# A decoder layer on one core: second norm, key choice and up products rearranged

## The chip, the cores and the metric

The kernel runs on 1 core of a Trainium2 chip (trn2). The metric is the device time of one execution in microseconds (us); the time before is the median of three runs. One execution was also taken by the hardware profiler, and all rows below come from its trace. Engines: PE is TensorE's matmul, PEld its weight load, DVE is VectorE, ACT ScalarE, POOL GpSimd, SP SyncE.

## The reference

One layer over 256 tokens of width 2048, in float32. The part that matters here is what follows the token mixer:

```python
x = x + gate1 * token_mixer(h, ...)
h = rmsnorm(x, norm2_g[l]) * (1.0 + scale2) + shift2
x = x + gate2 * peer(h, peer_w_q[l], peer_sub_keys[l], peer_w_up[l], peer_w_down[l])

def peer(h, w_q, sub_keys, w_up, w_down):
    qp = (h @ w_q).reshape(B, S, 8, 2, 128)
    s = jnp.einsum('bshpe,hpne->bshpn', qp, sub_keys)
    v1, i1 = lax.top_k(s[..., 0, :], 16)
    v2, i2 = lax.top_k(s[..., 1, :], 16)
    cand = (v1[..., :, None] + v2[..., None, :]).reshape(B, S, 8, 256)
    top, ci = lax.top_k(cand, 16)
    e1 = jnp.take_along_axis(i1, ci // 16, axis=-1)
    e2 = jnp.take_along_axis(i2, ci % 16, axis=-1)
    idx = e1 * 128 + e2
    g = jax.nn.softmax(top, axis=-1)
    # per token: y = sum over its 128 experts of g * gelu(h . w_up[idx]) * w_down[idx]
```

The second factors of the modulation, scale2 and shift2, come from a product of the conditioning vector with w_ada.

## The kernel before, in words

Weights are streamed: a unit of 1 MB is loaded by SyncE into one of four buffers and split in two halves. Each half is cast by ScalarE to a high part (`split_a`, L84), VectorE or GpSimd takes the low part (`split_b`, L88), and TensorE multiplies high by high, high by low and low by high. `Stream.run` writes the order out by hand: the cast of a half is issued three halves ahead of its product. One product half is a tick; `st.at(d, f)` issues f d ticks later, ahead of that tick's product, and `st.spread` hands small steps to VectorE between ticks, as many as a budget allows. Every engine works through its queue in the order of issue.

**Second norm.** `out_done(n)` ends block n of the output projection: VectorE makes the new residual, ScalarE its sum of squares (L960). The turning of a block to columns, `tr` (L967 to L975), ends in ScalarE copies of PSUM to x1T; that of block 3 is kept as `x1c["last"]`. After the stream has been drained, `h2_start` finishes the factor A2, and `h2` sums the squares (L1021), takes the root on ScalarE (L1022) and the reciprocal, and spreads it over the partitions by a product with ones (L1029, L1031). `chunks(q)` then scales two columns blocks (L1039, VectorE), adds the bias on ScalarE (L1042, the high part) and takes the low part on VectorE (L1044). Chunks 0 and 1 come first, then `x1c["last"]`, then chunks 2 and 3; the others follow one pair a tick. After that the PSUM pool of the first phase is closed and that of the second opened over it; the query products (L1101 to L1105) write to the latter.

**Queries and keys.** `open_p2`, six ticks on, lets GpSimd issue the DMA of the keys (L1069). Query block n has 8 halves of 24 matmuls; `q_done` copies it out. After block 0, `keys_t` turns the keys on TensorE (L1083, 16 transposes through two PSUM buffers, copied out by ScalarE, L1084), and `scores` multiplies queries by keys (L1125), which starts the background search for the 16 largest.

**Key choice.** In `topk`, for each token half, each key half q and each half of the heads, VectorE compares the chosen place's key number with 0 to 15 (L1208), multiplies the result with the key indices (L1211) and sums over the last axis (L1213). Both operations have 1024 two-byte elements a partition. Meanwhile the up products of quarter 0 run: for each half VectorE turns the weights (L1255), ScalarE casts, GpSimd takes the low part.

**Up products.** `up_unit(q, r)` is one row of 128 experts in two halves of 8 column blocks. For q of 0 and 1, `mm` issues three matmuls of 256 columns for each block (L1270 to L1272), two rows share one PSUM tile, and `up_done` applies gelu straight from it. For q of 2 and 3, `mm_wide` multiplies the high weights with high and low activations in one matmul of 512 columns (L1282) and the low weights in one of 256 (L1287); `add_up` copies one half of the PSUM tile out on ScalarE (L1297) and adds the other on VectorE (L1300) before gelu. In quarter 1 the first 18 rows (`nsolo`) run alone, and the other 14 alternate with the down products of quarter 0.

Of the kernel before, what the change touches and what calls it, by code (L numbers as in the profile page):

```python
# [13 lines left out]
AF = mybir.ActivationFunctionType  # L14
OP = mybir.AluOpType
# [51 lines left out]
def layer_kernel(ctx, tc, x, c, norm1_g, norm2_g, w_ada, b_ada, w_in, conv_dw, conv_db, conv_ln_g,  # L67
                 conv_ln_b, w_conv_out, b_conv_out, q_norm_g, k_norm_g, w_attn_o, w_out, peer_w_q,
                 peer_sub_keys, peer_w_up, peer_w_down, out):
    nc = tc.nc  # L70
# [168 lines left out]
    st = Stream()  # L239
# [25 lines left out]
    eps_col = consts.tile([P, 1], F32, name="eps_col")  # L265
# [36 lines left out]
    A2 = consts.tile([P, NK], F32, name="A2")  # L302
# [60 lines left out]
    ssq = pc1.tile([P, 2], F32, name="ssq")  # L363
# [332 lines left out]
    def gate_done(which, ch):  # L696
# [4 lines left out]
                                    gate_b[which][:, 4 * ch:4 * ch + 4], op=OP.add)  # L701
        return done

    def mod2_done(dst, bias_at, ch):
        rows32 = slice(32 * ch, 32 * ch + 32)

        def done(acc):
            ps = tt_([P, NK], "mod2ps")
            for j in range(NK):
                nc.tensor.matmul(ps[rows32, j:j + 1], lhsT=acc[:, 0, 32 * j:32 * j + 32], rhs=ones[:, 0:1],  # L710
                                 start=True, stop=True)
            nc.vector.tensor_tensor(dst[rows32, :], ps[rows32, :], cols[rows32, bias_at:bias_at + 16], op=OP.add)
        return done

    gate_b = [cols2[:, 48:64], cols2[:, 64:80]]
# [231 lines left out]
    def out_done(n):  # L947
        view = lambda v: v.rearrange("p (i j l) -> p j i l", i=4, j=4)
        of_row = lambda v: v.rearrange("p (i n j l) -> p n j i l", i=4, n=4, j=4)[:, n]

        def done(z):
            og = []
            for t in range(2):

                o = t2k("og")
                ov = o.rearrange("p (j i l) -> p j i l", i=4, j=4)
                nc.vector.tensor_tensor(ov, view(z[t]), of_row(mT["g1"]), op=OP.mult)
                nc.vector.tensor_tensor(ov, ov, of_row(x1c["t"][:, t]), op=OP.add)
                junk = wk.tile([P, 512], F32, name="junk2", tag="yc")
                nc.scalar.activation(junk, o, AF.Square, accum_out=ssq2[:, t, n:n + 1])  # L960
                nc.gpsimd.dma_start(x1_dram[:, t, n * 512:(n + 1) * 512], o)
                og.append(o)
            if n == 0:
                for i in range(2):
                    x1c[i] = wk.tile([P, 8, T], F32, name="x1T", tag="c8" + "bc"[i])

            def tr():  # L967
                for m in range(2):
                    pt = tt_([P, 2, T], "px")
                    for kk in range(2):  # L970
                        for t in range(2):
                            nc.tensor.transpose(pt[:, kk, t * P:(t + 1) * P],
                                                og[t][:, (2 * m + kk) * P:(2 * m + kk + 1) * P], ident)
                    at = 4 * (n % 2) + 2 * m
                    nc.scalar.copy(x1c[n // 2][:, at:at + 2, :], pt)  # L975
            if n < 3:
                st.at(2, tr)
            else:
                x1c["last"] = tr
        return done  # L980
# [34 lines left out]
    def h2_start():  # L1015
        nc.vector.tensor_scalar(A2, A2, 1.0, None, op0=OP.add)
        nc.vector.tensor_tensor(A2, A2, cols[:, 64:80], op=OP.mult)

    def h2():
        r2 = pc1.tile([P, 2], F32, name="r2")  # L1020
        nc.vector.tensor_reduce(r2, ssq2, axis=AX, op=OP.add)  # L1021
        nc.scalar.activation(r2, r2, AF.Sqrt, scale=1.0 / D, bias=eps_col)  # L1022
        nc.vector.reciprocal(r2, r2)

        diag = wk.tile([P, T], F32, name="diag", tag="ln", bufs=2)
        for t in range(2):
            nc.vector.tensor_scalar(diag[:, t * P:(t + 1) * P], ident, r2[:, t:t + 1], None, op0=OP.mult)
        pr = tt_([P, T], "rms")
        nc.tensor.matmul(pr, lhsT=ones, rhs=diag, start=True, stop=True)  # L1029
        rr = wk.tile([P, T], F32, name="rrow", tag="ln", bufs=2)  # L1030
        nc.scalar.copy(rr, pr)  # L1031

        qh["t"] = main.tile([P, NK, 2, T], F32R, name="h2", tag="hT")
        qh["hi"], qh["lo"] = qh["t"][:, :, 0], qh["t"][:, :, 1]

        def chunks(q):
            tmp = t2k("h2t").rearrange("p (c t) -> p c t", c=2)
            for c in range(2):
                nc.vector.scalar_tensor_tensor(tmp[:, c], x1c[(q + c) // 8][:, (q + c) % 8, :], A2[:, q + c:q + c + 1], rr,  # L1039
                                               op0=OP.mult, op1=OP.mult)  # L1040
            for c in range(2):
                nc.scalar.activation(qh["hi"][:, q + c, :], tmp[:, c], AF.Identity, bias=B2[:, q + c:q + c + 1])  # L1042
            for c in range(2):
                nc.vector.scalar_tensor_tensor(qh["lo"][:, q + c, :], tmp[:, c], B2[:, q + c:q + c + 1],  # L1044
                                               qh["hi"][:, q + c, :].bitcast(F32), op0=OP.add, op1=OP.subtract)

        for q in range(0, NK, 2):
            if q == 2:
                x1c["last"]()
            if q < 4:  # L1050
                chunks(q)
            else:
                st.at(q // 2 - 2, lambda q=q: chunks(q))
        ps0.close()
        T2["ps"] = p2.enter_context(tc.tile_pool(name="psq", bufs=1, space=PSUM))
        T2["psy"] = p2.enter_context(tc.tile_pool(name="psy", bufs=1, space=PSUM))

        def rest():
            pm.close()
            p1.close()  # L1060
            open_p2()
        st.at(6, rest)
# [50 lines left out]
    def q_done(n, ps):  # L1113
        scr = T2["scr"]
        qpT = scr[:, 4096:8192].rearrange("p (a t) -> p a t", a=16)
        for b in range(2):
            nc.scalar.copy(qpT[:, 4 * n + 2 * b:4 * n + 2 * b + 2, :], ps[b])
        if n == 0:
            st.at(1, keys_t)

        def scores():
            for t in range(2):
                pt = T2["ps"].tile([P, 4, P], F32, name="sps", tag="m", bufs=2)
                for a in range(4):
                    nc.tensor.matmul(pt[:, a, :], lhsT=qpT[:, 4 * n + a, t * P:(t + 1) * P],  # L1125
                                     rhs=T2["keysT"][:, (4 * n + a) * P:(4 * n + a + 1) * P], start=True, stop=True)
                nc.scalar.copy(scr[:, t * 2048 + n * 512:t * 2048 + (n + 1) * 512], pt.rearrange("p a n -> p (a n)"))
            st.spread(topk_keys(n))
            if n == 3:
                st.spread(topk_gen)  # L1130
        st.at(3, scores)


    def top16(rows_, cost):
# [27 lines left out]
    def topk():  # L1162
        scr = T2["scr"]
        small, big = (T2["pool"].tile([P, 768], F32, name=f"small{i}", tag="ohg", bufs=2) for i in range(2))
        iota16 = small[:, 0:128].bitcast(BF).rearrange("p (a k) -> p a k", a=16)
        nc.gpsimd.iota(iota16, pattern=[[0, 16], [1, 16]], base=0, channel_multiplier=0,
                       allow_small_or_imprecise_dtypes=True)
        idb = small[:, 128:256].bitcast(BF).rearrange("p (g a) -> p g a", a=TOPK)
        cab = small[:, 256:384].bitcast(BF).rearrange("p (q h a) -> p q h a", q=2, a=TOPK)
# [7 lines left out]
        for t in range(2):  # L1177
# [26 lines left out]
            i4 = idb.rearrange("p (h q) a -> p h q a", q=2)  # L1204
            shape = [P, H8 // 2, TOPK, TOPK]
            for q in range(2):
                for hs in halves:
                    nc.vector.tensor_tensor(eq[:, hs], cab[:, q, hs, :, None].to_broadcast(shape),  # L1208
                                            iota16[:, None, :, :].to_broadcast(shape), op=OP.is_equal)
                    yield 0.7, 0  # L1210
                    nc.vector.tensor_tensor(pr[:, hs], eq[:, hs], i4[:, hs, q, None, :].to_broadcast(shape), op=OP.mult)  # L1211
                    yield 1.2, 0
                    nc.vector.tensor_reduce(ee[:, q, hs], pr[:, hs], axis=AX, op=OP.add)  # L1213
                    yield 1.2, 0
# [23 lines left out]
    def up_unit(q, r, pool_lo):  # L1238
# [11 lines left out]
        for n in range(2):  # L1250
# [55 lines left out]
                    st.at(1, add)  # L1306

            h.a, h.b, h.mm = a, b, mm
            if q >= 2:
                h.mm = mm_wide  # L1310
                if n == 1:
                    h.after = [add_up]
            elif n == 1 and r % 2 == 1:
                h.after = [lambda: up_done(q, r - 1, C["ps"])]
            u.halves.append(h)
        return u

    NT = 8  # L1320
# [6 lines left out]

    def up_rows(q, r):

        if q == 2:  # L1330
            return c_row(q, r, 2).rearrange("p (r t) -> p r t", r=2)
        return T2["pool"].tile([P, 768], F32, name="hrow", tag="ohg", bufs=2)[:, 0:512].rearrange("p (r t) -> p r t", r=2)
# [25 lines left out]
    def weigh(upto):  # L1358
        while late and late[0][0] < upto:
            late.pop(0)[1]()  # L1360
# [204 lines left out]
    some = lambda r, n: n == 1 and r % 2 == 1  # L1565
    add_units([up_unit(0, r, busy) for r in range(EQ)])
    mark_up1 = len(st.halves)
    nsolo = 18
    solo = [up_unit(1, r, busy) for r in range(nsolo)]
    for u in solo:  # L1570
        for h in u.halves:
# [43 lines left out]
    st.run(mark_h2)  # L1615
    st.flush()
    st.finish()
    h2_start()
    h2()
    st.run(mark_up)  # L1620
    st.rate = 1.35
# [44 lines left out]
```

## Time and profile before

| | us |
|---|---|
| median of three runs | 2495.65 (2494.63 to 2496.32) |
| the profiled execution | 2495.79 |
| its span, first to last instruction | 2494.0 |

The page of the profile gives the busy time of each engine and the costliest groups of instructions. The view of stretches gives the busy time by engine in a window, then the granted clock of TensorE, the busy share of the DMA engines and their rate. In the timeline each row is a start and a duration in us, the engine, the line, the operation and its tiles, and in brackets how long the engine had been idle and what ended that. A matmul's recorded duration overlaps the next one's, so the pace of matmuls is read from their starts.

### The profile page before, as it was taken

To read this page: it belongs to the slowest core of one execution; us is meant where nothing else is said; L and a number is where in the kernel's file an instruction comes from. 1 tells how busy PE (TensorE), PEld (TensorE's weight loads), DVE (VectorE), ACT (ScalarE), POOL (GpSimd) and SP (SyncE) were. 2 spreads that over 40 slices of the span, in tenths; PEclk is the share of its full clock that TensorE was granted. 3 is DMA by queue.
4 is the path that set the end of the run, shared out by engine and by line. 5 is a ranking of instruction groups with operands and counts; after the bars stand their busy time and mean duration, and the time that the engine had idled before them with its cause. 6 is when DMAs were issued, how large, how long until landed. Compare 5 with 4: busy or idle time off the path is not lost.

```text
span 2494.0 us, 37872 instructions
## 1 busy us (share of the span) xinstructions
PE 2420.0 (97%) x14704; PEld 2007.3 (80%) x14704; DVE 1874.4 (75%) x2706; ACT 1141.0 (46%) x1540; POOL 525.5 (21%) x262
## 2 busy tenths in 40 slices
PE   7999999999999899988999999999999999999998
PEld 4677877777777799888889988888877888888877
DVE  2655788787564589897998777888899777776766
ACT  5333544444434444343335555555443444455454
POOL 1000000000000008776642233322000111133023
PEclk9999999999999899999999999999999999999999
DMA  9887457677898768676557876899844687766553
GB/s 332 299 304 253 152 203 260 246 272 248 285 289 242 162 158 185 149 162 143 119 136 215 231 225 190 225 235 232 213 142 145 177 198 182 187 193 220 187 201 118
DMA packets 261172, 518.62 MB, mean 208 GB/s; under 512 B 16400, under 2 KB 57568, under 8 KB 260352
## 3 DMA queue, kind: packets, MB, share of 16 engines
q1 hardware_dynamic: 258912, 507.61, 69.8%
q0 software_dynamic: 2048, 8.58, 1.0%
q8 instruction: 115, 1.88, 0.3%
q14 instruction: 65, 0.53, 0.1%
q10 hardware_dynamic: 32, 0.01, 0.0%
HBM read 511.94 MB, written 4.19 MB: 207 GB/s over the span
## 4 chain that ended last, share of the span: by engine, by line
PE 81%; DVE 8%; POOL 1%; issue 1%; ACT 1%; DMA 0%; DVEq 0%; SPq 0%; POOLq 0%; ACTq 0%
PE aps L1282 9%; PE y L1484 6%; PE y L1485 6%; PE y L1487 6%; PE z L429 5%; PE z L431 5%; PE z L430 5%; PE aps L1287 5%; PE z L1485 3%; PE z L1484 3%; PE z L1487 3%; PE aps L1272 3%; PE aps L1270 3%; PE aps L1271 3%; PE ada L330 2%; DVE wt L1255 2%
## 5 line engine op out<-in xcount | busy, mean ns | idle before, releaser
L88 DVE TENSOR_TENSOR lo<-raw,hi 128x1024 fp32r<-128x1024 f32 x456 | 560.1, 1233 | 318.7 <-issue 92.0
L84 ACT CAST hi<-raw 128x1024 fp32r<-128x1024 f32 x504 | 526.9, 1052 | 483.4 <-DMA raw<-in_w_in_dram 92.5
L84 ACT CAST hi<-wt 128x1024 fp32r<-128x1024 f32 x256 | 269.3, 1052 | 443.1 <-DVE wt L1255 427.5
L88 POOL TENSOR_TENSOR lo<-wt,hi 128x1024 fp32r<-128x1024 f32 x116 | 290.6, 2511 | 609.4 <-PE aps L1287 420.4
L1282 PE MATMUL aps<-h,hi 128*128 128x512 f32 x1024 | 362.4, 399 | 0.0
L1255 DVE STREAM_TRANSPOSE wt<-raw 128x1024 f32<-128x1024 f32 x256 | 315.3, 1235 | 26.5 <-POOL lo L88 21.3
L1272 PE MATMUL aps<-h,lo 128*128 128x256 f32 x1024 | 293.3, 286 | 11.8 <-POOL lo L88 11.8
L1270 PE MATMUL aps<-h,hi 128*128 128x256 f32 x1024 | 295.8, 289 | 0.0
L1271 PE MATMUL aps<-h,hi 128*128 128x256 f32 x1024 | 292.2, 285 | 0.0
L1467 DVE TENSOR_TENSOR ccl<-C,cch 128x256 fp32r<-128x256 f32 x248 | 197.0, 796 | 112.3 <-PE z L1487 59.1
L1287 PE MATMUL aps<-h,lo 128*128 128x256 f32 x1024 | 277.2, 281 | 0.0
L1484 PE MATMUL y<-hi,cch 128*128 128x512 f32 x608 | 241.1, 397 | 0.0
L1485 PE MATMUL y<-lo,cch 128*128 128x512 f32 x608 | 236.9, 390 | 0.0
L1282 PEld LDWEIGHTS aps<-h,hi 128*128 128x128 f32 x1024 | 190.3, 188 | 42.7 <-issue 0.2
L1272 PEld LDWEIGHTS aps<-h,lo 128*128 128x128 f32 x1024 | 198.9, 194 | 13.8 <-POOL lo L88 13.8
L1270 PEld LDWEIGHTS aps<-h,hi 128*128 128x128 f32 x1024 | 199.0, 194 | 1.2 <-ACT hi L84 0.5
L1271 PEld LDWEIGHTS aps<-h,hi 128*128 128x128 f32 x1024 | 199.3, 195 | 0.5
L1287 PEld LDWEIGHTS aps<-h,lo 128*128 128x128 f32 x1024 | 193.3, 189 | 6.3 <-issue 0.2
L88 DVE TENSOR_TENSOR lo<-wt,hi 128x1024 fp32r<-128x1024 f32 x140 | 175.3, 1255 | 19.3 <-PE aps L1287 12.2
L1487 PE MATMUL y<-hi,ccl 128*128 128x512 f32 x608 | 187.5, 389 | 0.0
L88 POOL TENSOR_TENSOR lo<-raw,hi 128x1024 fp32r<-128x1024 f32 x48 | 116.9, 2435 | 247.4 <-PE z L1485 125.2
L1462 ACT CAST cch<-C 128x256 fp32r<-128x256 f32 x248 | 99.8, 403 | 122.0 <-PE z L1485 103.4
(304 smaller groups left out, 4530.5 us busy)
## 6 DMA issues: line engine op xcount, KB each, us to landing
raw<-in_peer_w_up_dram SPq DMA_DIRECT2D x512, 256.0 KB, 5.8
raw<-in_peer_w_down_dram SPq DMA_DIRECT2D x128, 1024.0 KB, 5.2
raw<-in_w_ada_dram SPq DMA_DIRECT2D x86, 1024.0 KB, 6.9
raw<-in_w_in_dram SPq DMA_DIRECT2D x73, 1024.0 KB, 6.9
raw<-in_w_out_dram SPq DMA_DIRECT2D x64, 256.0 KB, 5.0
raw<-in_peer_w_q_dram SPq DMA_DIRECT2D x64, 256.0 KB, 6.2
raw<-in_w_in_dram SPq DMA_DIRECT2D x22, 512.0 KB, 9.1
raw<-in_w_ada_dram SPq DMA_DIRECT2D x20, 512.0 KB, 4.9
```

Source lines behind the costliest of these rows:

```text
L84: nc.scalar.copy(h.hi, src)
L88: eng.tensor_tensor(h.lo, src, h.hi.bitcast(F32), op=OP.subtract)
L1255: nc.vector.transpose(wt.rearrange("p j g a -> p g j a"), u.raw.rearrange("p (g j a) -> p g j a", g=4, a=32)[:, :, n * 8:(n + 1) * 8, :])
L1270: nc.tensor.matmul(z, lhsT=hi[:, jj], rhs=qh["hi"][:, j, :], start=j == 0, stop=False)
L1271: nc.tensor.matmul(z, lhsT=hi[:, jj], rhs=qh["lo"][:, j, :], start=False, stop=False)
L1272: nc.tensor.matmul(z, lhsT=lo[:, jj], rhs=qh["hi"][:, j, :], start=False, stop=j == NK - 1)
L1282: wide = lambda: nc.tensor.matmul(z.rearrange("p a t -> p (a t)"), lhsT=hi[:, jj], rhs=qh["t"][:, j].rearrange("p a t -> p (a t)"), start= ...
L1287: nc.tensor.matmul(z[:, 0], lhsT=lo[:, jj], rhs=qh["hi"][:, j, :], start=False, stop=False, skip_group_check=True)
L1467: nc.vector.tensor_tensor(cl, row, ch, op=OP.subtract)
L1484: nc.tensor.matmul(z, lhsT=ch, rhs=hi, start=first, stop=False)
L1485: nc.tensor.matmul(z, lhsT=ch, rhs=lo, start=False, stop=False)
L1487: nc.tensor.matmul(z, lhsT=cl, rhs=hi, start=False, stop=last)
```

## The change

`h2_start` is called when the last of the four A2 chunks is done, in `mod2_done`, and no longer after the drain. After block 2 of the output projection, ScalarE takes the root of a constant, so that the table for roots is loaded there. Chunks 0 and 1 of the norm go through all three steps one after the other, in place of step by step together. The turning of the keys is due three ticks after block 0 and no longer one, the scores of block 0 four ticks after it and no longer three. In the key choice the compare has the places innermost, the key number being the outer axis; the multiplication reads in that order and writes with the last two axes exchanged, so the sum reads as before. Rows 18 to 31 of quarter 1 use the wide product, whose sums land in the H buffer.

```diff
@@ mod2_done
+    mod2_left = [4, 4]
             nc.vector.tensor_tensor(dst[rows32, :], ps[rows32, :], cols[rows32, bias_at:bias_at + 16], op=OP.add)
+            if dst is A2:
+                mod2_left[0] -= 1
+                if mod2_left[0] == 0:
+                    h2_start()
@@ out_done
+            if n == 2:
+                nc.scalar.activation(ssq[:, 0:1], eps_col, AF.Sqrt)
@@ h2
-        def chunks(q):
+        def chunks(q, one=False):
             tmp = t2k("h2t").rearrange("p (c t) -> p c t", c=2)
-            for c in range(2):
+            if one:
+                for c in range(2):
+                    part(tmp, q, (c,))
+            else:
+                part(tmp, q, range(2))
+
+        def part(tmp, q, cc):
+            for c in cc:
                 nc.vector.scalar_tensor_tensor(tmp[:, c], x1c[(q + c) // 8][:, (q + c) % 8, :], A2[:, q + c:q + c + 1], rr,
                                                op0=OP.mult, op1=OP.mult)
-            for c in range(2):
+            for c in cc:
                 nc.scalar.activation(qh["hi"][:, q + c, :], tmp[:, c], AF.Identity, bias=B2[:, q + c:q + c + 1])
-            for c in range(2):
+            for c in cc:
                 nc.vector.scalar_tensor_tensor(qh["lo"][:, q + c, :], tmp[:, c], B2[:, q + c:q + c + 1],
                                                qh["hi"][:, q + c, :].bitcast(F32), op0=OP.add, op1=OP.subtract)
...
-                chunks(q)
+                chunks(q, q == 0)
@@ q_done
-            st.at(1, keys_t)
+            st.at(3, keys_t)
...
-        st.at(3, scores)
+        st.at(4 if n == 0 else 3, scores)
@@ topk
-        nc.gpsimd.iota(iota16, pattern=[[0, 16], [1, 16]], base=0, channel_multiplier=0,
+        nc.gpsimd.iota(iota16, pattern=[[1, 16], [0, 16]], base=0, channel_multiplier=0,
...
-                    nc.vector.tensor_tensor(eq[:, hs], cab[:, q, hs, :, None].to_broadcast(shape),
-                                            iota16[:, None, :, :].to_broadcast(shape), op=OP.is_equal)
+                    nc.vector.tensor_tensor(eq[:, hs], cab[:, q, hs, None, :].to_broadcast(shape),
+                                            iota16[:, None].to_broadcast(shape), op=OP.is_equal)
                     yield 0.7, 0
-                    nc.vector.tensor_tensor(pr[:, hs], eq[:, hs], i4[:, hs, q, None, :].to_broadcast(shape), op=OP.mult)
+                    nc.vector.tensor_tensor(pr[:, hs].rearrange("p h k a -> p h a k"), eq[:, hs],
+                                            i4[:, hs, q, :, None].to_broadcast(shape), op=OP.mult)
@@ up_unit
-            if q >= 2:
+            if q >= 2 or (q == 1 and r >= nsolo):
                 h.mm = mm_wide
@@ up_rows
+        if q == 1:
+            weigh(r - 14)
+            return C["H"][:, r % 16:r % 16 + 2]
@@ the order at the end
-    h2_start()
+    assert mod2_left[0] == 0
     h2()
```

## Rows read from the trace of the kernel before

**Rows 1.** The page: busy time by engine; the casts of the stream.

```profile
PE 2420.0 (97%) x14704; PEld 2007.3 (80%) x14704; DVE 1874.4 (75%) x2706; ACT 1141.0 (46%) x1540; POOL 525.5 (21%) x262
...
L84 ACT CAST hi<-raw 128x1024 fp32r<-128x1024 f32 x504 | 526.9, 1052 | 483.4 <-DMA raw<-in_w_in_dram 92.5
```

**Rows 2.** Stretches: window, length, busy PE, PEld, DVE, ACT, POOL, clock, DMA.

```profile
820.00:830.00 10.00, 4.09 (x15) 2.92 (x14) 5.89 (x16) 5.61 (x12) 1.08 (x2) 0.69 0.76 175
1060.00:1120.00 60.00, 53.53 (x432) 52.00 (x431) 56.49 (x88) 24.33 (x26) 46.20 (x19) 1.00 0.70 159
1300.00:1400.00 100.00, 100.00 (x631) 90.94 (x630) 83.15 (x82) 54.59 (x76) 24.81 (x15) 1.00 0.78 228
```

**Rows 3.** Timeline of the norm; then the table load of the attention roots, by line.

```profile
823.17 1.28 ACT L1022 ACT_TABLE_LOAD   x1
823.19 0.16 DVE L1021 TENSOR_REDUCE r<-ssq 128x2 f32<-128x8 f32 x1 [0.55 <-ACT junk L960]
...
827.26 0.88 DVE L1039 SCALAR_TENSOR_TENSOR h2t<-x1T,A,rrow 128x256 f32<-128x256 f32 x2 [1.78 <-ACT rrow L1031]
...
828.33 0.88 DVE L1044 SCALAR_TENSOR_TENSOR h<-h2t,B,h 128x256 fp32r<-128x256 f32 x2 [0.18 <-ACT h L1042]
828.60 1.05 ACT L975 COPY x1T<-px 128x512 f32<-128x512 f32 x2
...
829.70 0.29 PEld L1101 LDWEIGHTS qp<-h,hi 128*128 128x128 f32 x1 [1.57 <-ACT x1T L975]
...
L493 ACT ACT_TABLE_LOAD  x1: 1283/1283/1283, 283.3 to 283.3; - x1
```

**Rows 4.** Timeline around the turning of the keys; its sequencer's wait, by line.

```profile
850.46 1.18 POOL L1069 DMA_DIRECT2D C<-in_peer_sub_keys_dram  x1 [27.29 <-DVE h L1044]
...
857.45 0.28 PE L1105 MATMUL qp<-h,lo 128*128 128x256 f32 x1
863.26 3.73 PE L1083 MATMUL kt<-ident,C 128*128 128x128 f32 x16 [5.53 <-issue]
866.64 0.56 PE L1101 MATMUL qp<-h,hi 128*128 128x256 f32 x1
...
868.21 0.28 PE L1103 MATMUL qp<-h,hi 128*128 128x256 f32 x1
...
L1083 PEldq EVENT_SEMAPHORE  x4: 51/51/7452, 855.4 to 863.1; - x4
```

**Rows 5.** Timeline: narrow and wide products; the add, by line (min/median/max ns).

```profile
1426.14 0.28 PE L1270 MATMUL aps<-h,hi 128*128 128x256 f32 x1
...
1431.54 0.28 PE L1270 MATMUL aps<-h,hi 128*128 128x256 f32 x1
...
1599.94 0.40 PE L1282 MATMUL aps<-h,hi 128*128 128x512 f32 x1
...
1605.60 0.40 PE L1282 MATMUL aps<-h,hi 128*128 128x512 f32 x1
...
L1300 DVE TENSOR_TENSOR C<-aps,C x32: 409/415/420, 1575.5 to 1831.2; 128x256 f32<-128x256 f32 x32
```

**Rows 6.** Timeline of one choice (GpSimd alone, then merged); waits in 1000 to 1120.

```profile
1016.10 1.23 DVE L1255 STREAM_TRANSPOSE wt<-raw 128x1024 f32<-128x1024 f32 x1
1016.28 2.35 POOL L88 TENSOR_TENSOR lo<-wt,hi 128x1024 fp32r<-128x1024 f32 x1 [2.92 <-PE aps L1271]
...
1016.28 5.70 POOL L88 TENSOR_TENSOR lo<-wt,hi 128x1024 fp32r<-128x1024 f32 x2 [2.92 <-PE aps L1271]
1017.25 2.47 DVE L1208 TENSOR_TENSOR C<-small 128x1024 bf16<-128x1024 bf16 x1
1019.75 2.78 DVE L1211 TENSOR_TENSOR C<-C,small 128x1024 bf16<-128x1024 bf16 x1
...
1024.71 1.22 DVE L1255 STREAM_TRANSPOSE wt<-raw 128x1024 f32<-128x1024 f32 x1
...
PE aps L1272 <- POOL lo L88: 11.8, 9, 1.9
```

More of the change, by code (lines that the diff above doesn't have):

```diff
@@ L1316, in up_unit @@
         return u
+    nsolo = 18
     NT = 8
@@ L1567, in layer_kernel @@
     mark_up1 = len(st.halves)
-    nsolo = 18
     solo = [up_unit(1, r, busy) for r in range(nsolo)]
```

## The prediction

> **What bounds the kernel now.** I read the page first: TensorE is busy for 97% of the span, VectorE for 75% and ScalarE for 46% [rows 1]. So time can be won only where TensorE stands idle or runs slowly, or by giving it less to do. The view of stretches says where to look [rows 2]. In 820 to 830 us, the second norm, TensorE is busy for 4.09 of 10 us, at a granted clock of 0.69; in 1060 to 1120 us, where the top 16 are chosen, it loses 6.5 of 60 us while VectorE is busy for 56.5. In 1300 to 1400 us, where the rows that become wide lie, it is busy throughout: there only less work on TensorE counts. The timeline adds a pause of 5.5 us at 863 us, ahead of the turning of the keys [rows 4]. The change touches all four places. Times below are of the profiled execution, 2495.8 us with 2494.0 of span; it stands 0.1 us above the median, so its sum is also the median's.
>
> **The norm: root table early, chunks one by one.** On the chain [rows 3], ScalarE, done with its last sum of squares, loads the table for the root from 823.17 to 824.45, and the root follows at about 824.47. The sum that it needs (L1021) ends at 823.35. With the table loaded after block 2, the root can start about 0.05 us after that, at 823.40: 1.07 us won. The load itself moves to a stretch where ScalarE has time (46% busy in all [rows 1]); casts run three halves ahead of TensorE there, so I cost it at nothing, or 1.28 us if that lead were gone. Squares of block 3 follow it: in the attention part a single load [rows 3] serves the twelve roots that `qk_done` takes (L493), with Squares between them, so no second load is due. The two steps that finish A2 (16 columns each) stand on VectorE ahead of L1021, which waits for ScalarE's sum anyway; moving them to the last A2 chunk is worth 0, and there they stand between ordinary VectorE work.
>
> The chunks then give the gain back. What the first weight load of the queries waits for is not chunk 0 but the copies of x1T out of PSUM: it starts at 829.70, 0.05 us after these end at 829.65 [rows 3]. On ScalarE the copies are queued behind the bias step of chunk 1. Now VectorE scales chunks 0 and 1 back to back at 827.26 and about 827.66. One by one, it scales chunk 0, waits for ScalarE's bias step, takes the remainder of chunk 0 at 828.33 and only then, some 0.40 us later (0.88 us for a pair less 0.48 for one), scales chunk 1, at 828.73: 1.07 us later than now. The bias step of chunk 1, the copies behind it and the first weight load all move with it. So 1.07 - 1.07 = 0 for the whole norm; the bounds are -1.1 (the load doesn't really wait for the copies) and +0.4 (one more VectorE step ahead of the copies).
>
> **Keys turned later.** The ninth half of the query product ends at 857.57 (its last matmul starts at 857.45), and the turning of the keys starts only at 863.26. Its sequencer waits for 7.45 us from 855.4, until about 862.9, for the keys: GpSimd issues their DMA at 850.46, after VectorE has read the last old tile [rows 4]. The turning then runs slowly until 866.64, and so do the next products: seven starts from there to 868.21 take 1.57 us where 0.12 each [rows 5] makes 0.84. So 857.57 to 866.64 is 9.07 us, and with the slow start 9.8. The change lets two halves (24 x 0.12 = 2.88 us each) run first: 857.57 + 5.76 = 863.33, just behind the landing. Nothing issued before 863 us moves: the next release of a weight buffer would come after 864. Then the turning runs warm: 16 transposes of about 0.11 us, with a pause for the copies (two buffers; 0.53 us each by the pair of the same size in [rows 3]), which now stand behind a cast of 1.05 us on ScalarE, by its mean on the page (1052 ns [rows 1]). I get 1.05 + 0.53 + 0.1 = 1.7 us to the third group, and two groups of 0.5 with a short wait: 2.7 us. 9.8 - 2.7 = **7.1 us won**. If the keys land 1 us later, 6.1; if the copies never hold TensorE up, 8.0. The scores of block 0 come one half later behind the stream but some 4 us earlier by the clock; the background work of VectorE that they start has room before block 1's scores. Who waits behind the turning is TensorE alone.
>
> **Wide up products.** A half of 24 narrow products starts at 0.36 us for each three, and the wide form at about 0.354 us for each two: from 1426.14 to 1431.54 there are 15 threes (5.40 us), from 1599.94 to 1605.60 sixteen twos (5.66 us, so 15 of them 5.31) [rows 5]. That is 0.006 us x 16 x 14 rows = 1.4 us. Added are 14 copies on ScalarE, which has time, and 14 adds on VectorE (0.42 us, one operand in PSUM) [rows 5]: 5.9 us of VectorE in some 170 us in which it is about 83% busy [rows 2]. The cover is its free sixth, so I cost them at nothing; without it they would cost 5.9. **1.2 us won** after a little for the first rows; bounds 1.6 won and, without the cover, 4.5 lost, which nothing here points to.
>
> **The key choice.** This is the large unknown. Eight times (two token halves, two keys, two halves of the heads) VectorE compares (L1208), multiplies (L1211) and sums. Both operations read two operands from SBUF and wait for the GpSimd subtraction in progress, and the next subtraction waits for them. In the group at 1017.25 [rows 6] the compare waits for the subtraction that started at 1016.28 and lasts 2.35, until 1018.63, and runs until 1019.72, 1.09 us; the next subtraction follows it; the multiplication waits for that, until 1021.98 (the two end 5.70 after 1016.28), and ends at 1022.53, a run of 0.55 us. The two runs show the rates: the compare repeats one operand along its innermost axis and takes 1.06 ns an element, the multiplication has unit steps and takes 0.53. The group from 1016.10 to 1024.71, 8.6 us, holds two halves of 2.88 us of TensorE, and TensorE waits for GpSimd's remainder in each (11.8 us in nine waits in 1000 to 1120 us [rows 6]). VectorE is the bound in these groups, so a change of its own run falls on TensorE in full, eight times.
>
> After the change the compare has unit steps: 0.55 us. The multiplication repeats its index operand and, in addition, writes 16 places apart, two bytes at a time. Call its run P. The sum is 8 x (0.55 + P - 1.09 - 0.55) = 8 x (P - 1.09). The ends: 0.55 (today's multiplication; -4.3 us) and 2.78 (the longest time that one took here, wait included; +13.5 us). The nearest row is the compare of today, 1.09, but that has one operand off unit steps and a dense output, and the new multiplication has two off. The one row that compares such forms shows a doubling for one; I take a doubling for each: P = 2.13, **8.3 us lost**. That the waits shift with the shorter compare adds some 2 us either way.
> [...]
>
> **Sum.** 0 - 7.1 - 1.2 + 8.3 = 0.0: 2495.8 us, no change. About 5 us (0.2%) is what a measurement of this kernel can tell from none.
>
> **Rivals.**
> 1. The scattered write costs nothing extra: P = 1.09, the compare and the multiplication only change places. Then -7.1 - 1.2 = -8.3, 2487.5 us. [...] It decides below P = 1.5 (8 x 0.41 = 3.3, net -5).
> 2. Slower, by the write alone: from P = 2.75 on, 8 x 1.66 = 13.3 outweighs 8.3 by 5 us: 2501 us. For it: GpSimd is held off for all of P, and its subtraction is next on the path of every half. Against it: nothing of this size is seen in a run of VectorE here.
> 3. Slower, by the keys: the keys' DMA shares the engines with the weight loads, and lands with TensorE's progress rather than by the clock. If 5.5 us of the wait stays, net is -1.6 - 1.2 + 8.3 = +5.5: 2501.3 us. Against it: no load is issued earlier than now before the keys have landed.
> 4. The norm doesn't do what it says, or does: 0 is my sum, -1.1 the gain without the chunks' delay; 2494.7 us.
>
> **How the numbers follow.** The forecast (P from 1.5 to 2.75, with rival 4 in it) has 0.53; rival 1 has 0.30; rivals 2 and 3 have 0.12 and 0.05. So faster by over 0.2% 0.30, within it 0.53, slower 0.17. The forecast's own range is 2490.8 to 2500.8 us. The range of 8 in 10 takes in the time of rival 1 (2487.5, with half a microsecond for its other terms) and reaches on the other side to 2502.
>
> **What would show it.** Right: the new multiplication runs about 2.1 us beyond the end of GpSimd's operation, the compare 0.55; TensorE's waits for GpSimd's remainder in 1000 to 1120 us grow from 11.8 to about 20 us; no idle time before the turning of the keys, and 7 us less in 853 to 876 us; the first weight load of the queries still at 829.7, right behind the copies of x1T, though the root is at 823.4. Wrong: a multiplication of 1.1 us beyond the wait (then 2487), or a first weight load near 828.6. Idle time before the turning, or TensorE waits in 1300 to 1475 us, would say that the keys or the wide rows were mis-sized.

## The result, and the profile after

The changed kernel takes 2515.1 us (median of six runs, 2513.0 to 2517.7), the kernel before 2496.0 beside it: a ratio of 1.0083, interval 1.0070 to 1.0095. It is 19 us slower; 2495.8 was forecast, with 2502 as the upper end. One of the six runs of the kernel before took 9864 us and the other five 2492.0 to 2498.0, so that its median is hardly moved by the one. The profiled execution took 2512.95 us, 2511.2 of it span, and so lies 2.2 us below the median.

The busy line of the page of after, beside [rows 1]:

```profile
PE 2425.3 (97%) x14480; PEld 2002.1 (80%) x14480; DVE 1903.4 (76%) x2720; ACT 1145.1 (46%) x1555; POOL 535.0 (21%) x262
```

TensorE has 224 matmuls fewer, as meant, and VectorE is busy for 29 us longer. The two stretches of after that hold the norm and the choice, beside [rows 2] (window, length, busy time of each engine, clock, DMA):

```profile
820.00:830.00 10.00, 4.11 (x16) 2.92 (x15) 5.75 (x14) 4.32 (x11) 1.08 (x2) 0.70 0.92 209
1060.00:1120.00 60.00, 51.55 (x384) 50.58 (x383) 57.66 (x94) 21.93 (x24) 48.57 (x17) 0.91 0.68 156
```

In 1060 to 1120 us TensorE gets through 384 matmuls where it had 432, at a granted clock of 0.91 where it was 1.00, and VectorE is busy for 57.66 of the 60 us. One key choice of after, on the timeline of VectorE, GpSimd and ScalarE in turn, and under them TensorE's waits in 1000 to 1120 us (total us, times, longest), beside [rows 6]. L1272 turns weights, L1224 is the compare, L1227 the multiplication, L1230 the sum, L84 the cast, L88 the remainder:

```profile
1016.31 1.22 DVE L1272 STREAM_TRANSPOSE wt<-raw 128x1024 f32<-128x1024 f32 x1
1017.46 1.94 DVE L1224 TENSOR_TENSOR C<-small 128x1024 bf16<-128x1024 bf16 x1
1019.43 6.62 DVE L1227 TENSOR_TENSOR C<-C,small 128x1024 bf16<-128x1024 bf16 x1
1025.68 1.43 DVE L1272 STREAM_TRANSPOSE wt<-raw 128x1024 f32<-128x1024 f32 x1
1027.05 1.16 DVE L1230 TENSOR_REDUCE small<-C 128x64 f32<-128x1024 bf16 x1
1028.14 1.21 DVE L1272 STREAM_TRANSPOSE wt<-raw 128x1024 f32<-128x1024 f32 x1
...
1016.50 5.14 POOL L88 TENSOR_TENSOR lo<-wt,hi 128x1024 fp32r<-128x1024 f32 x2 [6.68 <-ACT hi L84]
1028.32 5.15 POOL L88 TENSOR_TENSOR lo<-wt,hi 128x1024 fp32r<-128x1024 f32 x2 [6.68 <-ACT hi L84]
...
1027.20 1.04 ACT L84 CAST hi<-wt 128x1024 fp32r<-128x1024 f32 x1 [8.03 <-DVE wt L1272]
...
PE aps L1289 <- POOL lo L88: 16.2, 8, 3.0
PE aps L1287 <- ACT hi L84: 4.5, 2, 2.3
```

GpSimd's second subtraction ends at 1016.50 + 5.14 = 1021.64, the multiplication at 1026.05: a run of 4.41 us of its own, where the prediction had 2.13 and at most 2.78. The group takes 1016.31 to 1028.14, 11.8 us instead of 8.6. The brackets show the way to TensorE: the transposition of the next weights is queued behind the multiplication, ScalarE's cast stands idle for 8.03 us for it, GpSimd for 6.68 us for the cast, and TensorE now waits for both. The sign that the prediction named, TensorE's waits in 1000 to 1120 us growing to about 20 us, came true (16.2 + 4.5 = 20.7) though the choice loses more than three times the 8.3 us forecast for it: TensorE does less of its work in that window (728 matmuls, before 863), and a part of the loss is no wait, as the next table's stage b to c shows.

To see where the span went I divide it by four starts of TensorE: a the first query product, b the last product of queries by keys, c the last transposition of chosen places, d the first of the products into y at L1528 (L1507 before). They are the first and the last start in these rows of the view by line, of after (min/median/max ns, then first to last start):

```profile
L1117 PE MATMUL qp<-h,hi x256: 278/283/579, 829.8 to 931.7; 128*128 128x256 f32 x128
L1141 PE MATMUL sps<-C,C x64: 271/275/377, 869.1 to 934.2; 128*128 128x128 f32 x64
L1237 PE MATMUL eT<-ident,small x2: 273/273/273, 1051.4 to 1150.7; 128*128 128x128 f32 x2
L1528 PE MATMUL y<-raw,C x64: 592/592/673, 1861.4 to 1969.2; 128*128 128x512 f32 x64
```

The same rows of every kernel, those of the experiments below included, give in us of its profiled execution:

| kernel | to a | a to b (queries, keys) | b to c (choice) | c to d (up products) | d to the end | span |
|---|---|---|---|---|---|---|
| before | 829.7 | 111.4 | 188.8 | 712.5 | 651.6 | 2494.0 |
| after | 829.8 | 104.4 | 216.5 | 710.7 | 649.8 | 2511.2 |
| A_no_choice | 830.7 | 103.9 | 187.1 | 714.4 | 651.4 | 2487.5 |
| B_choice_only | 832.2 | 111.6 | 216.4 | 712.4 | 651.7 | 2524.3 |
| C_dense | 829.7 | 104.3 | 189.0 | 709.5 | 651.3 | 2483.8 |
| D_four_byte | 831.7 | 104.0 | 193.7 | 710.6 | 649.7 | 2489.7 |
| E_norm_pair | 828.5 | 104.3 | 187.1 | 709.4 | 651.4 | 2480.7 |
| H_keys_early | 830.5 | 111.7 | 189.0 | 708.7 | 651.3 | 2491.2 |
| F_pair_compare | 829.0 | 103.7 | 187.0 | 716.6 | 651.3 | 2487.6 |

From before to after: +0.1, -7.0, +27.7, -1.8 and -1.8 make +17.2 us. All but the choice went as forecast, or better. The column c to d wanders between 708.7 and 716.6 us in kernels that have the same code there; TensorE's waits for masks that VectorE makes are 6.2 us in H and 11.3 us in F, a part of that. A difference of a few us between two medians can come from there, so the stages are what I compare below.

The stage b to c holds the same work of TensorE before and after. The view of stretches for it, of before and then of after (columns as in [rows 2]):

```profile
941.10:1129.90 188.80, 177.03 (x1425) 174.38 (x1424) 166.54 (x305) 77.17 (x85) 147.88 (x60) 0.98 0.74 166
934.20:1150.70 216.50, 187.48 (x1424) 184.29 (x1423) 194.30 (x305) 77.05 (x84) 158.31 (x60) 0.92 0.64 145
```

TensorE's idle time grows from 11.8 to 29.0 us, which is 17.2 of the 27.7 us; in the other 10.5 us it is busy for longer with the same 1424 matmuls. The granted clock goes with that: 0.92 in place of 0.98. Behind a wait that ends at 1018.90 us its matmuls start 0.21 us apart for a while (twelve steps from 1019.28 to 1021.84), at a granted clock of 0.50 there, and 0.12 us apart after that, at 1.00 from 1022 to 1024 us. Waits alone show too little of such a loss. How much of the slower clock would have counted if VectorE had not been the bound, no run separates.

### The profile page after: what moved, and what is told of

It reads as the page before. It is cut to its first block, busy times and chain, and to the rows that moved or that the text cites. A ratio compares the mean times of both kernels' runs of the same rounds, so it can differ in the third digit from the quotient of the medians.

```text
span 2511.2 us, 37453 instructions
## 1 busy us (share of the span) xinstructions
PE 2425.3 (97%) x14480; PEld 2002.1 (80%) x14480; DVE 1903.4 (76%) x2720; ACT 1145.1 (46%) x1555; POOL 535.0 (21%) x262
## 4 chain that ended last, share of the span: by engine, by line
PE 77%; DVE 9%; issue 2%; POOL 2%; DMA 1%; ACT 1%; SPq 0%; DVEq 0%; ACTq 0%; POOLq 0%
PE aps L1299 12%; PE aps L1304 6%; PE y L1505 6%; PE y L1506 5%; PE y L1508 5%; PE z L429 5%; PE z L431 5%; PE z L430 5%; PE z L1506 3%; PE z L1505 3%; PE z L1508 3%; DVE wt L1272 2%; PE ada L330 2%; POOL lo L88 2%; DVE oh L1401 2%
## 5 line engine op out<-in xcount | busy, mean ns | idle before, releaser
L88 DVE TENSOR_TENSOR lo<-raw,hi 128x1024 fp32r<-128x1024 f32 x456 | 558.2, 1229 | 307.9 <-issue 98.4
L84 ACT CAST hi<-raw 128x1024 fp32r<-128x1024 f32 x504 | 527.0, 1052 | 474.2 <-PE aps L1299 89.8
L84 ACT CAST hi<-wt 128x1024 fp32r<-128x1024 f32 x256 | 269.3, 1052 | 472.0 <-DVE wt L1272 445.4
L1299 PE MATMUL aps<-h,hi 128*128 128x512 f32 x1248 | 442.7, 399 | 0.0
L88 POOL TENSOR_TENSOR lo<-wt,hi 128x1024 fp32r<-128x1024 f32 x116 | 301.0, 2602 | 619.6 <-PE aps L1304 420.4
L1272 DVE STREAM_TRANSPOSE wt<-raw 128x1024 f32<-128x1024 f32 x256 | 316.5, 1239 | 28.4 <-POOL lo L88 24.7
L1299 PEld LDWEIGHTS aps<-h,hi 128*128 128x128 f32 x1248 | 232.4, 188 | 52.3 <-issue 0.2
L1287 PE MATMUL aps<-h,hi 128*128 128x256 f32 x800 | 236.9, 296 | 8.9 <-ACT hi L84 8.9
L1288 PE MATMUL aps<-h,hi 128*128 128x256 f32 x800 | 233.1, 291 | 0.0
L88 DVE TENSOR_TENSOR lo<-wt,hi 128x1024 fp32r<-128x1024 f32 x140 | 174.8, 1251 | 17.0 <-PE aps L1304 11.0
L88 POOL TENSOR_TENSOR lo<-raw,hi 128x1024 fp32r<-128x1024 f32 x48 | 116.9, 2436 | 245.5 <-PE z L1506 123.6
L1287 PEld LDWEIGHTS aps<-h,hi 128*128 128x128 f32 x800 | 161.3, 202 | 9.9 <-ACT hi L84 9.9
L1288 PEld LDWEIGHTS aps<-h,hi 128*128 128x128 f32 x800 | 161.0, 201 | 0.0
```

The costliest lines, as they stand in the source:

```text
L84: nc.scalar.copy(h.hi, src)
L88: eng.tensor_tensor(h.lo, src, h.hi.bitcast(F32), op=OP.subtract)
L1272: nc.vector.transpose(wt.rearrange("p j g a -> p g j a"), u.raw.rearrange("p (g j a) -> p g j a", g=4, a=32)[:, :, n * 8:(n + 1) * 8, :])
L1287: nc.tensor.matmul(z, lhsT=hi[:, jj], rhs=qh["hi"][:, j, :], start=j == 0, stop=False)
L1288: nc.tensor.matmul(z, lhsT=hi[:, jj], rhs=qh["lo"][:, j, :], start=False, stop=False)
L1299: wide = lambda: nc.tensor.matmul(z.rearrange("p a t -> p (a t)"), lhsT=hi[:, jj], rhs=qh["t"][:, j].rearrange("p a t -> p (a t)"), start= ...
```

## The experiments

### The choice undone, and the choice alone

A_no_choice is the kernel after with three statements of the choice as before:

```diff
-        nc.gpsimd.iota(iota16, pattern=[[1, 16], [0, 16]], ...)
+        nc.gpsimd.iota(iota16, pattern=[[0, 16], [1, 16]], ...)
-        nc.vector.tensor_tensor(eq[:, hs], cab[:, q, hs, None, :].to_broadcast(shape), iota16[:, None].to_broadcast(shape), ...)
+        nc.vector.tensor_tensor(eq[:, hs], cab[:, q, hs, :, None].to_broadcast(shape), iota16[:, None, :, :].to_broadcast(shape), ...)
-        nc.vector.tensor_tensor(pr[:, hs].rearrange("p h k a -> p h a k"), eq[:, hs], i4[:, hs, q, :, None].to_broadcast(shape), ...)
+        nc.vector.tensor_tensor(pr[:, hs], eq[:, hs], i4[:, hs, q, None, :].to_broadcast(shape), ...)
```

> The changed kernel with the key choice as it was before: only the norm, the keys and the wide rows are left of the change. Theory 1 (the scattered product of the key choice is the whole loss): the other parts give what was summed, 7.1 for the keys and 1.2 for the wide rows, so 2496.0 - 8.3 = 2487.7 us. Theory 2 (another part loses as well, or the keys give nothing): between 2496 and 2513 us.

Measured: 2489.5 us, ratio 0.9969 (0.9957 to 0.9981). B_choice_only is the kernel before with the opposite edit.

> The kernel before with the new key choice alone. Theory 1: the multiplication runs about 4.4 us beyond the end of GpSimd's subtraction (seen in the changed kernel) in place of 0.55, the compare 0.55 in place of 1.09, so 8 x (4.4 - 1.09) = 26 us: 2522 us. Theory 2: much less, at most 2505 us, and the rest of the loss needs the other parts.

Measured: 2522.5 us, ratio 1.0100 (1.0086 to 1.0115). The multiplication of B (ns):

```profile
L1211 DVE TENSOR_TENSOR C<-C,small x8: 5679/6455/6625, 1005.4 to 1138.0; 128x1024 bf16<-128x1024 bf16 x8
```

The choice alone loses 26 us (2522.5 less 2496.1 beside it), the rest alone wins 7. In the table the stage b to c has 216.5 and 216.4 us with the new choice, 187.1 and 188.8 without. The whole loss is the choice's.

### Which part of the multiplication is dear

The new multiplication differs in two things: its index operand is repeated, and its result is scattered. C_dense keeps the first and drops the second; the sum then adds the wrong elements and the experts are wrong, so this kernel serves for its time alone. D_four_byte keeps both, and widens what is written.

```diff
@@ C_dense
-        nc.vector.tensor_tensor(pr[:, hs].rearrange("p h k a -> p h a k"), eq[:, hs],
+        nc.vector.tensor_tensor(pr[:, hs], eq[:, hs],
                                 i4[:, hs, q, :, None].to_broadcast(shape), op=OP.mult)
@@ D_four_byte
-            pr = scr[:, 7168:8192].bitcast(BF).rearrange("p (h a k) -> p h a k", h=H8, a=TOPK)
+            pr = scr[:, 4096:6144].rearrange("p (h a k) -> p h a k", h=H8, a=TOPK)
```

> The changed kernel with the product written in the order in which it is read, densely; the sum after it then adds the wrong elements, and the experts chosen are wrong. Theory 1 (the write that steps 16 places is dear): the multiplication runs 1.1 us, as the old compare with its one repeated operand did, and the time is 2488 to 2490 us. Theory 3 (the repeated index operand is dear): it still runs 4.4 us, and the time stays at 2513 to 2515 us.

> The changed kernel with the product in four-byte elements, still written 16 places apart (64 bytes). Theory 1a (two-byte pieces make the scattered write dear): the run falls to 2.2 us or less, and the time to 2497 us or less. Theory 1b (any write that jumps at every element costs this): the run stays at 4 us or more, and the time at 2513 us or above.

Measured: C 2486.0 us, ratio 0.9959 (0.9944 to 0.9973); D 2496.5 us, ratio 0.9993 (0.9979 to 1.0007). One group of C, then one of D, each with the subtractions beside it:

```profile
1010.86 1.93 DVE L1224 TENSOR_TENSOR C<-small 128x1024 bf16<-128x1024 bf16 x1
1012.82 3.31 DVE L1227 TENSOR_TENSOR C<-C,small 128x1024 bf16<-128x1024 bf16 x1
...
1009.89 5.16 POOL L88 TENSOR_TENSOR lo<-wt,hi 128x1024 fp32r<-128x1024 f32 x2 [3.45 <-PE aps L1289]
```

```profile
1013.87 1.93 DVE L1224 TENSOR_TENSOR C<-small 128x1024 bf16<-128x1024 bf16 x1
1015.84 4.04 DVE L1227 TENSOR_TENSOR C<-C,small 128x1024 f32<-128x1024 bf16 x1
...
1012.90 5.18 POOL L88 TENSOR_TENSOR lo<-wt,hi 128x1024 fp32r<-128x1024 f32 x2 [4.08 <-ACT hi L84]
```

In C GpSimd ends at 1015.05 and the multiplication at 1016.13: 1.08 us of its own, the price with a repeated operand and a dense result. In D they end at 1018.08 and 1019.88: 1.80 us for results of four bytes, though they lie 64 bytes apart and no longer 32. So the scatter is the cause, and most of its price is that of two-byte pieces: 4.41 against 1.80. Over E, whose stage b to c has 187.1 us, the three runs P of 1.08, 1.80 and 4.41 us cost 1.9, 6.6 and 29.4 us. The prediction's 8 x (P - 1.09) gives 0, 5.7 and 26.6, short by 1 to 3 us: for these three runs the formula holds that well, and its P did not.

### The price of a hop by itself

G_probe is the kernel before with single operations on 1024 elements a partition at its end, after the last add, on data that nothing else uses. For each step of 2, 4, 8, 16 and 32 elements a product is read densely and written that many elements apart (`hop`), in two and then in four bytes; then both forms dense; then one of two sources read 16 apart; then copies.

```diff
+    hop = lambda v, s: v.rearrange("p (b k a) -> p b a k", k=16, a=s)
+    rd = lambda v, s: v.rearrange("p (b a k) -> p b a k", k=16, a=s)
...
+    nc.vector.tensor_tensor(hop(d2, 16), rd(s2, 16), rd(s2, 16), op=OP.mult)
...
+    nc.vector.tensor_tensor(hop(dst, 16), rd(src, 16), rd(src, 16), op=OP.mult)
...
+    nc.vector.tensor_tensor(d2, s2, s2, op=OP.mult)
...
+    nc.vector.tensor_tensor(rd(d2, 16), hop(s2, 16), rd(s2, 16), op=OP.mult)
...
+    nc.vector.tensor_copy(hop(d2, 16), rd(s2, 16))
+    nc.scalar.copy(hop(d2, 16), rd(s2, 16))
+    nc.scalar.copy(rd(d2, 16), rd(s2, 16))
```

> The kernel before with single VectorE operations on 1024 elements a row added at its end, where GpSimd has nothing to do: results in two bytes and in four bytes, written densely and at steps of several widths. Its own time is not compared. Theory 1: a two-byte result written 32 bytes apart takes about 4.4 us for 1024 elements with nobody beside it, a four-byte one 64 bytes apart about 1.8 us, dense ones about 1.1 us or less; so the loss is the price of the write by itself. Rival 1b: alone, the scattered two-byte write takes under 2.5 us, and the 4.4 us of the key choice come from what runs beside it there (GpSimd's operation, TensorE's copies).

Its timeline at the end, of one execution. L1644 to L1648 write two bytes at steps of 4, 8, 16, 32 and 64 bytes, L1649 to L1653 four bytes at steps of 8 to 128, L1654 and L1655 densely; L1656 reads two bytes 32 apart and writes densely; L1658 is VectorE's copy of two-byte elements, read densely and written 32 bytes apart; L1659 and L1660 are ScalarE's copies, both read densely, the first written 32 bytes apart and the second densely:

```profile
2496.08 1.30 DVE L1644 TENSOR_TENSOR pdst<-psrc 128x1024 bf16<-128x1024 bf16 x1
2497.41 2.40 DVE L1645 TENSOR_TENSOR pdst<-psrc 128x1024 bf16<-128x1024 bf16 x1
2499.85 4.69 DVE L1646 TENSOR_TENSOR pdst<-psrc 128x1024 bf16<-128x1024 bf16 x1
2504.57 4.44 DVE L1647 TENSOR_TENSOR pdst<-psrc 128x1024 bf16<-128x1024 bf16 x1
2509.04 4.60 DVE L1648 TENSOR_TENSOR pdst<-psrc 128x1024 bf16<-128x1024 bf16 x1
2513.68 1.23 DVE L1649 TENSOR_TENSOR pdst<-psrc 128x1024 f32<-128x1024 f32 x1
2514.93 1.97 DVE L1650 TENSOR_TENSOR pdst<-psrc 128x1024 f32<-128x1024 f32 x1
2516.94 2.00 DVE L1651 TENSOR_TENSOR pdst<-psrc 128x1024 f32<-128x1024 f32 x1
2518.97 1.88 DVE L1652 TENSOR_TENSOR pdst<-psrc 128x1024 f32<-128x1024 f32 x1
...
2522.82 0.69 DVE L1654 TENSOR_TENSOR pdst<-psrc 128x1024 bf16<-128x1024 bf16 x1
2523.55 1.22 DVE L1655 TENSOR_TENSOR pdst<-psrc 128x1024 f32<-128x1024 f32 x1
2524.81 1.99 DVE L1656 TENSOR_TENSOR pdst<-psrc 128x1024 bf16<-128x1024 bf16 x1
...
2528.74 2.31 DVE L1658 COPY pdst<-psrc 128x1024 bf16<-128x1024 bf16 x1
2531.08 4.47 ACT L1659 COPY pdst<-psrc 128x1024 bf16<-128x1024 bf16 x1 [49.35 <-DVE pdst L1658]
2535.58 1.04 ACT L1660 COPY pdst<-psrc 128x1024 bf16<-128x1024 bf16 x1
```

With nobody beside it the write of the new choice (two bytes, 32 apart, L1647) takes 4.44 us, as it does in the choice (4.41). Rival 1b, contention with GpSimd, falls. The probe also parts what D changed together: at the same 64 bytes, two-byte results take 4.60 us (L1648) and four-byte ones 1.88 (L1652), so it is the size of the pieces and not their distance; D's 1.80 us, with sources of two bytes, says the same of the destination. But the price is not the destination's alone: the copy with its one source writes the same two-byte pieces 32 bytes apart in 2.31 us (L1658), about half. Why, no run here shows.

### The norm: chunks 0 and 1 in step again

E_norm_pair is A_no_choice with one edit more.

```diff
-                chunks(q, q == 0)
+                chunks(q)
```

> The kernel after with the key choice as before, and the first two chunks of the norm in step again; the root's table stays early. Theory N1, by the prediction's sum (table early 1.07 us gained, one by one 1.07 us lost): the first weight load of the queries comes some 1 us sooner after the multiplication by the inverse root than in the kernel after (1.6 us instead of 2.65), and the time is 1.1 us below that of the kernel after with only the choice undone (2489.5), about 2488.4. Rival N2: TensorE's first products of the queries are followed by waits of their own, which take the gain back: the gap shortens, but the time stays at 2489.5.

Measured: 2484.6 us, ratio 0.9955 (0.9942 to 0.9968). The norm on the timeline, first of after, then of E:

```profile
823.34 0.16 DVE L1030 TENSOR_REDUCE r<-ssq 128x2 f32<-128x8 f32 x1 [0.85 <-ACT junk L966]
823.54 0.29 ACT L1031 ACTIVATE r<-r,eps_col 128x2 f32<-128x2 f32 x1 [0.23 <-DVE r L1030]
...
828.72 1.05 ACT L984 COPY x1T<-px 128x512 f32<-128x512 f32 x2
...
829.82 0.28 PEld L1117 LDWEIGHTS qp<-h,hi 128*128 128x128 f32 x1 [2.63 <-ACT x1T L984]
```

```profile
827.44 1.05 ACT L984 COPY x1T<-px 128x512 f32<-128x512 f32 x2
...
828.53 0.19 PEld L1117 LDWEIGHTS qp<-h,hi 128*128 128x128 f32 x1 [1.57 <-ACT x1T L984]
```

The copies end at 829.77 and 828.49, and the first weight load of the queries follows each by about 0.05 us. TensorE's idle time before it is 2.63 us with the chunks one by one and 1.57 in step: the 1.06 us that N1 expected. The median fell by 4.9 us against A, measured in another session; the ratios differ by 0.0014, about their intervals, and c to d alone differs by 5 us, so no more than the 1.06 us is the chunks'. E has both the early table and the chunks in step, and is the fastest kernel here, 0.45% below the kernel before.

### The keys at their early place

H_keys_early is A_no_choice with the turning one tick and the scores three ticks after block 0.

```diff
-            st.at(3, keys_t)
+            st.at(1, keys_t)
...
-        st.at(4 if n == 0 else 3, scores)
+        st.at(3, scores)
```

> The kernel after with the key choice as before, and the turning of the keys back at its early place. Theory K1, by the prediction: the idle time of TensorE ahead of the turned keys is back at about 5.5 us (0.24 in the kernel after), and the time is 7.1 us above that of the kernel after with only the choice undone, about 2496.6. Rival K2: the later place only exchanged one wait for another, and the time is within 2 us of 2489.5.

Measured: 2493.8 us, ratio 0.9998 (0.9987 to 1.0008), 0.0029 or 7 us above A's ratio; the two medians, of different sessions, are 4.3 us apart, and K1 had 2496.6 us. The turning in H, then, of after, the turning and its copies:

```profile
864.54 3.73 PE L1099 MATMUL kt<-ident,C 128*128 128x128 f32 x16 [5.95 <-issue]
```

```profile
863.90 1.07 PE L1099 MATMUL kt<-ident,C 128*128 128x128 f32 x8 [0.24 <-issue]
...
864.57 1.07 ACT L1100 COPY C<-kt 128x512 f32<-128x512 f32 x2
865.21 1.14 PE L1099 MATMUL kt<-ident,C 128*128 128x128 f32 x8 [0.24 <-ACT C L1100]
```

At the early place TensorE is idle for 5.95 us and then turns the keys in 3.73 us; at the later one it is idle for 0.24 us and turns them, copies between included, from 863.90 to 866.35. The stage a to b is 111.7 us in H and 103.9 in A: 7.8 us. By the stage and the idle time K1 stands, and with it falls the prediction's rival 3, by which the wait would have stayed.

### A faster compare

F_pair_compare is E with a compare whose operands have two neighbours side by side: each chosen number is stored twice.

```diff
-        nc.vector.tensor_copy(cab[:, 0], ca)
+        nc.vector.tensor_copy(cab[0], small[:, 384:512].bitcast(U32)[:, :, None].to_broadcast([P, 128, 2]))
...
+        nc.vector.tensor_tensor(eq[:, hs].rearrange("p h a (k j) -> p (h a) k j", j=2),
+                                cab[q][:, gs_, None, :].to_broadcast([P, 64, 8, 2]),
+                                iota16.rearrange("p (k j) -> p k j", j=2)[:, None].to_broadcast([P, 64, 8, 2]),
+                                op=OP.is_equal)
```

> The kernel with E's edits, and a comparison in the key choice whose operands are read with two neighbours side by side (each chosen number stored twice, the sixteen places in pairs); product and sum as in the kernel before. Theory F1: what makes the comparison of the kernel after short (648 ns alone, against 1182 in the kernel before) is that its operands are read in rows of neighbours, so the pairs bring most of it without the scattered write: about 0.5 us for each of 8, so 4 us less than E, less some 0.4 us for the longer copies, about 2485. Rival F2: the engine wants longer rows than two, the comparison stays at 1182 ns, and the time is E's or 0.4 us above it.

Measured: 2487.0 us, ratio 0.9967 (0.9956 to 0.9979), against E's 0.9955. The compare of E, then that of F (ns min/median/max):

```profile
L1224 DVE TENSOR_TENSOR C<-small x8: 1180/2378/2498, 993.0 to 1101.1; 128x1024 bf16<-128x1024 bf16 x8
```

```profile
L1225 DVE TENSOR_TENSOR C<-small x8: 648/1848/1952, 992.9 to 1100.0; 128x1024 bf16<-128x1024 bf16 x8
```

Each compare is 0.53 us shorter, so F1 is right about the operation; but the stage b to c has 187.0 us, E's 187.1, so the time was not won. VectorE's work became shorter and TensorE's waits did not: 9.2 us in E, 10.9 in F in 1000 to 1120 us, all for GpSimd's remainder. One group is shorter by as much, from one transposition to the next (8.60 us from 1008.05 in E, 8.10 us from 1007.42 in F), and the lead is gone by the end of the stage. What holds GpSimd there I did not test. The prediction counted the shorter compare of the new choice in full (8 x 0.54 = 4.3 us), and by F this is in doubt. Without it, 8 x (P - 0.55) gives 4.2, 10.0 and 30.9 us for C, D and after, over the measured 1.9, 6.6 and 29.4 by 1.5 to 3.4 us, so these runs do not decide between the two forms.

## Why the prediction was wrong, point by point

**The failed step** is the size of P, "a doubling for each: P = 2.13". Its own run is 4.41 us, 2.1 times what was taken and above the end of 2.78. Two things were wrong in how it was bounded. The upper end was the longest multiplication in the trace, wait included; but a row that has none of the operation in question bounds nothing, and all of those 2.78 us but its own 0.55 were a wait that the new multiplication has as well. And the doubling came from a repeated source, while what was new was the destination: C shows 1.08 us for a repeated source with a dense result, so the repeated source did cost what today's compare costs, and the scattered write made the rest, 3.33 us where its doubling had allowed about 1. (Two doublings of 0.55 us are 2.20 and not the recorded 2.13; over eight groups that is 0.6 us.) Rival 2 named the right cause, the write alone, with 0.12 and at 2501 us; at its measured price it is 26.6 us by the same formula. The way to TensorE is not quite the one that rival 2 gives: GpSimd is idle for 6.68 us for ScalarE's cast, and that waits for a transposition queued on VectorE behind the multiplication. Rival 1, a write that costs nothing extra, falls with the 4.41 us.

**That a change of VectorE's run falls on TensorE in full** held upward, within 1 to 3 us, as C, D and after show. Downward F speaks against it, where a shorter compare won nothing; by that a P at the lower end of 0.55 would hardly have won the 4 us that the formula gives it, which no run tried.

**The norm** was 0 by two equal terms, and was +0.1 us (the first weight load of the queries went from 829.70 to 829.82). The root starts at 823.54, 0.93 us before 824.47, and not at the 823.40 forecast, since the sum of squares came 0.15 us later; and E shows the 1.06 us that the chunks one by one give back. The step from x1T's copies to the first weight load was right.

**The keys** were forecast at 7.1 us and won 7.0 (a to b), 7.8 by A against H. The keys had landed, and the turning with its copies was put at 2.7 us; from 863.90 to 866.35 it is 2.45.

**The wide rows** were forecast at 1.2 us, and won 1.8, a little outside the bound of 1.6. From the first down product to the first wide product that before has as well, in before and then in after:

```profile
1302.08 0.40 PE L1484 MATMUL y<-hi,cch 128*128 128x512 f32 x1
...
1564.81 0.39 PE L1282 MATMUL aps<-h,hi 128*128 128x512 f32 x1
...
L1505 PE MATMUL y<-hi,cch x608: 389/389/796, 1322.9 to 2414.3; 128*128 128x512 f32 x152
...
1583.78 0.39 PE L1299 MATMUL aps<-h,hi 128*128 128x512 f32 x1
```

That is 262.7 us and then 260.9. The same stretch takes 260.9 us in all seven kernels above with the wide rows, and 262.7 in B, which has the narrow ones, so the gain is theirs; the wandering of c to d lies ahead of it. The adds on VectorE cost nothing that can be seen there.

By its own terms with the measured sizes the sum is 0.1 - 7.0 - 1.8 + 27.7 = +19.0 us, and a last 1.8 us less in d to the end, which D shares and whose cause I did not follow, makes the +17.2 of the two spans.

## What to carry to other kernels

Where the trace has no row of an operation's access form, the longest row of its kind is no upper bound (here 2.78 us, where 4.41 came): give that term a wide range and let it, not the well-measured terms, set the chances. Price the destination separately from the sources, by its element size (at steps of 64 bytes 4.60 us in two-byte elements, 1.88 in four-byte ones) and for the operation itself (two bytes at a time, 32 bytes apart, a copy took 2.31 us and a product of two sources 4.44); reading a scattered operand and writing densely was here the cheaper side (1.99 against 4.44 us). Read the granted clock beside the waits: here 10.5 of 27.7 us were the same matmuls taking longer. Undo a bundle's parts one at a time: three of these four were good or neutral, and the bundle without the other and with the pair in step beats both kernels.

## What the runs showed of the hardware

- In G a two-byte result of a product of two sources on VectorE took 0.69 us for 1024 elements written densely, 1.30 at a step of 4 bytes, 2.40 at 8, and 4.4 to 4.7 at 16, 32 and 64. A four-byte one took 1.22 densely, 1.23 at 8 bytes, and 1.88 to 2.00 at 16 to 128. A copy with one source, written two bytes at a time 32 bytes apart, took 2.31. Why two bytes are so much dearer no run here shows.
- ScalarE pays too: in G its copy of two-byte elements took 4.47 us written 32 bytes apart and 1.04 written densely, both read densely.
- In the choice of after TensorE's clock was granted at 0.92 on average against 0.98 before, where it waited for 29.0 us and not for 11.8: its matmuls of 256 columns started 0.21 us apart after a wait of 1.93 us, at a granted clock of 0.50, and 0.12 apart later, at 1.00.
- The shortest compare of F, whose repeated number is stored twice and read with two neighbours side by side, took 648 ns, as did that of after with the places innermost; that of E, with the number repeated along the innermost axis, took 1180.
